# Gate and up of each layer's first feed-forward part by seven block products

## The chip, the cores and the metric

The kernel runs on one core of a Trainium2 chip. TensorE (PE) multiplies, with weight loads shown as PEld; VectorE (DVE), ScalarE (ACT) and GpSimd (POOL) do elementwise work; SyncE (SP) issues most transfers. The metric is device time in microseconds. Three runs of the kernel before took 2079.54, 2082.31 and 2081.96 us; the median is 2081.96.

## The reference

Two layers, each of four residual updates on x (512 tokens, 1024 features, float32):

```python
x = x + 0.5 * _swiglu(_rms_norm(x, norm_ffn1[l]), ffn1_w_gate[l], ffn1_w_up[l], ffn1_w_down[l])
...
x = x + mix @ w_out[l]
x = x + 0.5 * _swiglu(_rms_norm(x, norm_ffn2[l]), ffn2_w_gate[l], ffn2_w_up[l], ffn2_w_down[l])
...
def _swiglu(x, w_gate, w_up, w_down):
    return (jax.nn.silu(x @ w_gate) * (x @ w_up)) @ w_down
```

D_FF is 2816. The mixer between the two feed-forward parts (recurrent heads, windowed attention, convolution) is not touched.

## The kernel before, in words

x lies transposed in SBUF: eight tiles x0 to x7 of 128 features by 512 tokens. Every float32 product is made of three fp32r products (mm3, L119 to L121): a matrix is split into hi (a rounded copy, by ACT) and lo (the rest, a subtraction by DVE), and hi·hi, hi·lo and lo·hi are added up in PSUM.

A feed-forward part walks over f, the 22 blocks of 128 columns of D_FF. For each f it takes two weight tiles of 128 x 1024 (gate, then up). slot (L105) loads one on SP's queue into raw, copies hi on ACT (L112) and subtracts lo on DVE (L113). Each has 8 k-tiles x 3 = 24 matmuls of 512 columns, so an f has 48. gated (L212) multiplies both results by R, the reciprocal norm of each token (DVE, L216 and L218), takes silu on ACT (L217), the product on POOL (L219), and splits it into ah and al (L124, L125). Then down: for each of the eight x tiles, 22 k-tiles x 3 matmuls in three loads, the sum added to x by DVE (L271).

The norm is put off: xh and xl are x times the norm's gains (norm_tile: ACT L172, DVE L173), and squares are summed on POOL (L181); norm_sum (L199) adds them over features, and norm_spread makes R. Since R is needed only at the gating, f = 0 can be multiplied before R is known. For the next part norm_tile runs tile by tile as down finishes each x.

At the start of layer 0 the loads are raw, x0, raw, x1 to x7; PE takes gate and up of f = 0 side by side, k-tile by k-tile, as xh and xl come in.

The order of work on each engine is settled when the kernel is built, by a scheduler that simulates it; every engine and every queue then takes its instructions in that order. Tiles with a fixed number of buffers (raw, hi and lo have three each) are handed on when their last reader is done.

Of the kernel before, what the change touches and what calls it, by code (L numbers as in the profile page):

```python
# [81 lines left out]
class Kern:  # L82
# [22 lines left out]
    def slot(self, src, cols, nm="w"):  # L105

        nc = self.nc
        raw = self.ring.tile([P, 1024], F32, tag="raw", name=self.n("raw"))
# [3 lines left out]
        nc.scalar.copy(hi[:, :cols], raw[:, :cols])  # L112
        nc.vector.tensor_tensor(lo[:, :cols], raw[:, :cols], hi[:, :cols].bitcast(F32), op=ALU.subtract)  # L113
# [42 lines left out]

    def norm_begin(self, idx):
        self.xp = self.tc.tile_pool(name=self.n("xp"), bufs=1, side="right")
        pool = self.xp.__enter__()
        xh = lambda j: pool.tile([P, T], F32R, tag=f"xh{j}", name=self.n("xh"))  # L160
        xl = lambda j: pool.tile([P, T], F32R, tag=f"xl{j}", name=self.n("xl"))
        self.xh, self.xl = [xh(j) for j in range(KT)], [xl(j) for j in range(KT)]
        pool.tile([P, XPAD], F32, name=self.n("xpad"))
        self.nidx = idx
        self.acc = self.nrm.tile([P, T], F32, tag="acc", name=self.n("acc"))

    def norm_tile(self, j):
# [4 lines left out]
        nc.scalar.activation(self.xh[j], x, AF.Copy, scale=g)  # L172
        nc.vector.scalar_tensor_tensor(  # L173
            self.xl[j], x, g, self.xh[j].bitcast(F32), op0=ALU.mult, op1=ALU.subtract
        )
        if j == 0:
            nc.scalar.activation(self.acc, x, AF.Square)
        else:
            sq = self.nrm.tile([P, T], F32, tag=("sq", "R")[j % 2], name=self.n("sq"))
            nc.scalar.activation(sq, x, AF.Square)  # L180
            nc.gpsimd.tensor_tensor(self.acc, self.acc, sq, op=ALU.add)  # L181
# [41 lines left out]

    def ffn(self, l, n, nxt, last=False):
        nc, I = self.nc, self.I
        with self.tc.tile_pool(name=self.n("ffn"), bufs=1) as ap, self.tc.tile_pool(name=self.n("fft"), bufs=2) as tp:
            ah, al = [], []
            held = None
            for f in range(FT):
                p = []  # L230
                if f == 0 and l == 0 and n == 0:

                    both = [self.ahead.pop(0) for w in range(2)]
                    p = [self.psum() for w in range(2)]
# [4 lines left out]
                    self.norm_sum()
                    held = p  # L240
                    continue
                for w in range(2):
# [795 lines left out]
    def run(self):  # L1038
        nc, tc, I = self.nc, self.tc, self.I
        self.consts()  # L1040
        self.x = []
        for j in range(KT):
            if j in (0, 1):
                self.ahead.append(self.slot(I["wgu"][0, 0, 0, j], 1024))
            self.x.append(self.xt(j))
            nc.sync.dma_start(out=self.x[j], in_=I["xT"][:, j])
# [85 lines left out]
```

## Time and profile before

| | us |
|---|---|
| median of three runs | 2081.96 |
| the profiled run's own time | 2079.0 |
| its span, first to last instruction | 2077.2 |
| PE busy | 2033.1 (98%) |
| DVE busy | 1122.4 (54%) |
| ACT busy | 743.7 (36%) |
| POOL busy | 335.5 (16%) |

A window row gives a stretch's start and end, its length, the busy time of PE, PEld, DVE, ACT and POOL with their instructions in brackets, the granted PE clock, the share of the DMA engines and their GB/s. A timeline row gives a start, a duration, the engine, the line, the operation, output<-inputs, shapes and count, and in square brackets the idle time before it with what ended it. A group row (by line and form) gives busy time and the mean in ns of one after the bar.

### The profile page before, as it was taken

How to read it: one execution, taken by the hardware profiler on the slowest of the kernel's cores; microseconds unless marked ns; L12 is line 12 of the kernel's file. 1: busy time of each engine (PE TensorE's matmuls, PEld its weight loads, DVE VectorE, ACT ScalarE, POOL GpSimd, SP SyncE). 2: the span in 40 equal slices, each digit the busy share in tenths (PEclk: the TensorE clock that was granted, in tenths of full speed). 3: DMA queues.
4: the chain of work that ended last, by engine and by line, in shares of the span. 5: the costliest groups of instructions: out<-in, count | busy, mean ns of one | idle time of the engine just before them, and what ended most of it. 6: DMA issues, size and time to landing. Idle time of an engine off the chain costs nothing. (4 is left out here: it accounts for less than half of the span.)

```text
span 2077.2 us, 26018 instructions
## 1 busy us (share of the span) xinstructions
PE 2033.1 (98%) x10406; PEld 1654.5 (80%) x10406; DVE 1122.4 (54%) x1565; ACT 743.7 (36%) x1136; POOL 335.5 (16%) x298
## 2 busy tenths in 40 slices
PE   8999999989999999999999999999899999999999
PEld 6888888768877788888888888887687677888887
DVE  5545433699766455543244554337997764454422
ACT  4332322454365332322232322325534653232221
POOL 3101101132411211110010111002323111110100
PEclk9999999999999999999999999999999999999999
DMA  4232333213212323233323232332133132333332
GB/s 169 92 102 93 95 109 124 80 57 92 78 42 89 109 92 99 94 97 100 98 91 102 92 101 89 120 112 90 44 92 90 33 105 92 94 100 102 99 109 66
DMA packets 81865, 193.80 MB, mean 93 GB/s; under 512 B 26640, under 2 KB 32272, under 8 KB 81744
## 3 DMA queue, kind: packets, MB, share of 16 engines
q1 hardware_dynamic: 81312, 191.79, 29.7%
q8 instruction: 81, 1.33, 0.3%
q10 hardware_dynamic: 432, 0.36, 0.1%
q14 instruction: 40, 0.33, 0.1%
HBM read 183.47 MB, written 8.65 MB: 92 GB/s over the span
## 5 line engine op out<-in xcount | busy, mean ns | idle before, releaser
L112 ACT CAST hi<-raw 128x1024 fp32r<-128x1024 f32 (+3 forms) x368 | 350.9, 954 | 991.0 <-PE psg L120 850.0
L113 DVE TENSOR_TENSOR lo<-raw,hi 128x1024 fp32r<-128x1024 f32 (+3 forms) x368 | 504.1, 1370 | 348.7 <-ACT hi L112 329.2
L119 PE MATMUL psg<-xh,hi 128*128 128x512 f32 x1632 | 642.9, 394 | 7.1 <-ACT xh L172 7.1
L120 PE MATMUL psg<-xl,hi 128*128 128x512 f32 x1632 | 641.1, 393 | 5.0 <-DVE xl L173 4.9
L121 PE MATMUL psg<-xh,lo 128*128 128x512 f32 x1632 | 641.0, 393 | 0.0
L120 PEld LDWEIGHTS psg<-xl,hi 128*128 128x128 f32 x1632 | 308.6, 189 | 74.3 <-DVE xl L173 8.9
L119 PEld LDWEIGHTS psg<-xh,hi 128*128 128x128 f32 x1632 | 308.6, 189 | 73.8 <-ACT xh L172 7.1
L121 PEld LDWEIGHTS psg<-xh,lo 128*128 128x128 f32 x1632 | 308.8, 189 | 66.4 <-issue 2.0
L119 PE MATMUL psg<-ah,hi 128*128 128x512 f32 x704 | 273.9, 389 | 0.0
L120 PE MATMUL psg<-al,hi 128*128 128x512 f32 x704 | 273.9, 389 | 0.0
L121 PE MATMUL psg<-ah,lo 128*128 128x512 f32 x704 | 273.9, 389 | 0.0
L219 POOL TENSOR_TENSOR s<-s,u 128x512 f32<-128x512 f32 x88 | 120.5, 1370 | 800.1 <-ACT hi L112 676.5
L218 DVE TENSOR_TENSOR u<-psg,R 128x512 f32<-128x512 f32 x88 | 60.8, 691 | 265.4 <-PE psg L121 265.1
L120 PEld LDWEIGHTS psg<-al,hi 128*128 128x128 f32 x704 | 132.2, 188 | 27.5
L121 PEld LDWEIGHTS psg<-ah,lo 128*128 128x128 f32 x704 | 132.2, 188 | 27.5
L119 PEld LDWEIGHTS psg<-ah,hi 128*128 128x128 f32 x704 | 132.2, 188 | 27.3
L216 DVE TENSOR_TENSOR g<-psg,R 128x512 f32<-128x512 f32 x88 | 60.8, 691 | 125.4 <-PE psg L121 125.4
L181 POOL TENSOR_TENSOR acc<-acc,sq 128x512 f32<-128x512 f32 x42 | 58.6, 1396 | 381.3 <-ACT sq L180 380.9
L1001 DVE SCALAR_TENSOR_TENSOR cacc<-z,par,cacc 128x482 f32<-128x482 f32 (+14 forms) x120 | 101.7, 847 | 1.7
L124 ACT CAST ah<-s 128x512 fp32r<-128x512 f32 x88 | 54.8, 623 | 121.7 <-POOL s L219 121.7
L125 DVE TENSOR_TENSOR al<-s,ah 128x512 fp32r<-128x512 f32 x88 | 59.8, 679 | 20.9 <-ACT ah L124 20.9
L867 PE MATMUL psg<-hi,xh 128*128 128x384 f32 x192 | 68.0, 357 | 1.3 <-ACT nat L892 1.3
(208 smaller groups left out, 1819.2 us busy)
## 6 DMA issues: line engine op xcount, KB each, us to landing
raw<-in_wgu_dram SPq DMA_DIRECT2D x176, 512.0 KB, 3.5
raw<-in_wd_dram SPq DMA_DIRECT2D x64, 512.0 KB, 3.5
raw<-in_win_dram SPq DMA_DIRECT2D x28, 512.0 KB, 3.5
raw<-in_wd_dram SPq DMA_DIRECT2D x32, 384.0 KB, 3.1
raw<-in_watt_dram SPq DMA_DIRECT2D x24, 384.0 KB, 3.0
raw<-in_wout_dram SPq DMA_DIRECT2D x28, 192.0 KB, 2.3
xs<-x SPq DMA_DIRECT2D x16, 256.0 KB, 2.0
x<-xs SPq DMA_DIRECT2D x16, 256.0 KB, 3.1
```

Of the source, the lines that this page charges most:

```text
L112: nc.scalar.copy(hi[:, :cols], raw[:, :cols])
L113: nc.vector.tensor_tensor(lo[:, :cols], raw[:, :cols], hi[:, :cols].bitcast(F32), op=ALU.subtract)
L119: mm(out, lhsT=whi, rhs=xhi, start=first, stop=False)
L120: mm(out, lhsT=whi, rhs=xlo, start=False, stop=False)
L121: mm(out, lhsT=wlo, rhs=xhi, start=False, stop=last)
L125: self.nc.vector.tensor_tensor(lo, src, hi.bitcast(F32), op=ALU.subtract)
L181: nc.gpsimd.tensor_tensor(self.acc, self.acc, sq, op=ALU.add)
L216: nc.vector.tensor_tensor(t[0], p[0], self.R, op=ALU.mult)
L218: nc.vector.tensor_tensor(t[1], p[1], self.R, op=ALU.mult)
L219: nc.gpsimd.tensor_tensor(t[2], t[2], t[1], op=ALU.mult)
L867: mm(o, lhsT=self.xh[kk][:, t], rhs=hi[:, s], start=kk == 0, stop=False)
L1001: nc.vector.scalar_tensor_tensor(a[:, d:], z[:, 0 : T - d], pa("dww", u * CW + j), a[:, d:], op0=ALU.mult, op1=ALU.add)
```

## The change

It concerns gate and up of the first feed-forward part of each layer. The second keeps the old scheme in ffn2, which now takes odd x tiles before even ones for gate's first half, since the weights' layout in memory changed.

The tokens are cut in two halves of 256 (t0, t1) and the k-tiles in even (e) and odd (o) ones. Per f the weights are four blocks of 128 x 512: a and b (gate, even and odd), c and d (up, even and odd). Instead of eight block products (four blocks, two token halves) seven are made, each of a sum of weight blocks with a form, a sum or difference of x's blocks: 4 k-tiles x 3 matmuls of 256 columns each, 84 per f. DVE adds the seven PSUM results up to gate (negated; silu then has scale -1) and up.

norm_forms replaces norm_tile's xh and xl here: for each pair of x tiles seven forms, as fh and fl. The weights go through stages, three items ahead: stage 1 (load) loads ba (b, a), s13 (a, c) and for two f at once dd (d) on SP. Stage 2 (sums1) adds (c, d) to s13 by an accumulating DMA from POOL's queue, and makes hi and lo of ba; lo is -hi by ACT to which a second accumulating DMA from POOL's queue adds ba (only the very first by DVE). Stage 3 (sums2) makes s24 by two DVE additions and hi and lo of s13 and s24; odd makes those of dd. The items are: up for f = 0 to 7, down with those eight for all x tiles, up 8 to 15, down, up 16 to 21, down with six. Each down adds its half of the sum to x, so x is added to three times. At the start of layer 0, ba, s13 and dd are loaded before x. The seven weight sums and forms of f = 0 are multiplied in the order 1, 5, then 6, 7, 2, 3 for three of the four pairs, then the fourth pair.

```diff
+HT = T // 2
+KP = KT // 2
+CH = 8
+ER = 3
+ES = 4
...
+        if idx % 3:
+            xh = lambda j: pool.tile([P, T], F32R, tag=f"xh{j}", name=self.n("xh"))
+            xl = lambda j: pool.tile([P, T], F32R, tag=f"xl{j}", name=self.n("xl"))
+            self.xh, self.xl = [xh(j) for j in range(KT)], [xl(j) for j in range(KT)]
+        else:
+            self.fh = [pool.tile([P, 7, HT], F32R, name=self.n("fh")) for _ in range(KP)]
+            self.fl = [pool.tile([P, 7, HT], F32R, name=self.n("fl")) for _ in range(KP)]
+            self.eo = pool.tile([P, 2, 2, HT], F32, name=self.n("eo"))
+            room = room or (lambda: pool.tile([P, T], F32, name=self.n("tf")))
+            self.tf = [room().rearrange("p (a c) -> p a c", a=2) for _ in range(2)]
         pool.tile([P, XPAD], F32, name=self.n("xpad"))
...
+    def norm_forms(self, j):
+        nc = self.nc
+        V, A = nc.vector, nc.scalar
+        g = self.nidx * KT + j
+        e, o, tf = self.eo[:, 0], self.eo[:, 1], self.tf
+        h, l = self.fh[j // 2], self.fl[j // 2]
+        f32 = lambda a: a.bitcast(F32)
+        x3 = self.x[j].rearrange("p (t c) -> p t c", t=2)
+        if j % 2 == 0:
+            A.activation(e, x3, AF.Copy, scale=self.gains[:, g : g + 1])
+            A.activation(h[:, 0], e[:, 0], AF.Copy, scale=-1.0)
+            V.tensor_tensor(tf[0][:, 0], e[:, 1], e[:, 0], op=ALU.subtract)
+            A.copy(h[:, 3], tf[0][:, 0])
+            V.scalar_tensor_tensor(l[:, 0], e[:, 0], -1.0, f32(h[:, 0]), op0=ALU.mult, op1=ALU.subtract)
+            V.tensor_tensor(l[:, 3], tf[0][:, 0], f32(h[:, 3]), op=ALU.subtract)
+        else:
+            A.activation(o, x3, AF.Copy, scale=self.gains[:, g : g + 1])
+            V.tensor_tensor(tf[0][:, 1], o[:, 1], tf[0][:, 0], op=ALU.subtract)
+            V.tensor_tensor(tf[1][:, 0], e[:, 1], o[:, 1], op=ALU.subtract)
+            V.tensor_tensor(tf[1][:, 1], o[:, 0], tf[0][:, 1], op=ALU.subtract)
+            A.activation(h[:, 1:3], o, AF.Copy, scale=-1.0)
+            V.scalar_tensor_tensor(l[:, 1:3], o, -1.0, f32(h[:, 1:3]), op0=ALU.mult, op1=ALU.subtract)
+            for a, t in ((slice(4, 5), tf[0][:, 1:2]), (slice(5, 7), tf[1])):
+                A.copy(h[:, a], t)
+                V.tensor_tensor(l[:, a], t, f32(h[:, a]), op=ALU.subtract)
...
-            self.xl[j], x, g, self.xh[j].bitcast(F32), op0=ALU.mult, op1=ALU.subtract
-        )
...
+            self.norm_forms(j)
         if j == 0:
...
+    def load(self, l, n, f):
+        w, k = self.I["wgu"], KP * P
+        v = lambda a: a.rearrange("p (x k) -> p x k", x=2)
+        ba = v(self.ring.tile([P, 1024], F32, tag="raw", name=self.n("ba")))
+        self.nc.sync.dma_start(out=ba, in_=v(w[l, n, f, :, 0 : 2 * k]))
+        s13 = self.ep.tile([P, 2, k], F32, tag="rs", name=self.n("s13"), bufs=ER)
+        self.nc.sync.dma_start(out=s13, in_=v(w[l, n, f, :, k : 3 * k]))
+        if f % 2 == 0:
+            self.dd = self.ep.tile([P, 2, k], F32, tag="rd", name=self.n("dd"))
+            self.nc.sync.dma_start(out=self.dd, in_=w[l, n, f : f + 2, :, 3 * k : 4 * k].rearrange("f p k -> p f k"))
+        return {"raw": (l, n, f, ba, s13), "dd": self.dd}
+    def parts(self, hi, lo, raw, dma=False):
+        nc = self.nc
+        nc.scalar.copy(hi, raw)
+        if dma:
+            nc.scalar.activation(lo, hi.bitcast(F32), AF.Copy, scale=-1.0)
+            nc.gpsimd.dma_start(out=lo, in_=raw, accum_op=ALU.add)
+        else:
+            nc.vector.tensor_tensor(lo, raw, hi.bitcast(F32), op=ALU.subtract)
+        return hi, lo
+    def two(self, pool, tag, bufs):
+        return [
+            pool.tile([P, 2, KP * P], F32R, tag=q + tag, name=self.n(q + tag), bufs=bufs)
+            for q in ("h", "l")
+        ]
+    def sums1(self, W):
+        l, n, f, ba, s13 = W["raw"]
+        k = KP * P
+        cd = self.I["wgu"][l, n, f, :, 2 * k : 4 * k].rearrange("p (x k) -> p x k", x=2)
+        self.nc.gpsimd.dma_start(out=s13, in_=cd, accum_op=ALU.add)
+        h, lo = (
+            self.ring.tile([P, 1024], F32R, tag=q, name=self.n(q), bufs=RB).rearrange("p (x k) -> p x k", x=2)
+            for q in ("hi", "lo")
+        )
+        self.parts(h, lo, ba, W["dma"])
+        W[1] = h[:, 1], lo[:, 1], 0
+        W[2] = h[:, 0], lo[:, 0], 1
+    def sums2(self, W):
+        V = self.nc.vector
+        l, n, f, ba, s13 = W["raw"]
+        s24 = self.ep.tile([P, 2, KP * P], F32, tag="rs", name=self.n("s24"), bufs=ER)
+        V.tensor_tensor(s24[:, 0], s13[:, 1], ba[:, 1], op=ALU.add)
+        V.tensor_tensor(s24[:, 1], s24[:, 0], ba[:, 0], op=ALU.add)
+        h, lo = self.parts(*self.two(self.ep, "s", ES), s13)
+        W[5] = h[:, 1], lo[:, 1], 3
+        W[7] = h[:, 0], lo[:, 0], 5
+        h, lo = self.parts(*self.two(self.ep, "s", ES), s24)
+        W[6] = h[:, 0], lo[:, 0], 4
+        W[3] = h[:, 1], lo[:, 1], 2
+    def odd(self, W):
+        f = W["raw"][2]
+        if f % 2 == 0:
+            self.hdd = self.parts(*self.two(self.ep, "d", 1), W["dd"])
+        W[4] = self.hdd[0][:, f % 2], self.hdd[1][:, f % 2], 6
...
+            def gated(f, g, u):
+                V.tensor_tensor(g, g, self.R, op=ALU.mult)
+                A.activation(g, g, AF.Silu, scale=-1.0)
+                V.tensor_tensor(u, u, self.R, op=ALU.mult)
+                G.tensor_tensor(g, g, u, op=ALU.mult)
+                ah[f] = ap.tile([P, T], F32R, tag=f"ah{f % CH}", name=self.n("ah"))
+                al[f] = ap.tile([P, T], F32R, tag=f"al{f % CH}", name=self.n("al"))
+                self.split(ah[f], al[f], g)
+            def up(f, W, held, then):
+                ps = {}
+                def mul(i, r=range(KP)):
+                    if i not in ps:
+                        ps[i] = self.psum(*(("b", 2) if i in (2, 7) else ()))[:, 0:HT]
+                    hi, lo, c = W[i]
+                    for p in r:
+                        s = slice(p * P, (p + 1) * P)
+                        self.mm3(ps[i], hi[:, s], lo[:, s], self.fh[p][:, c], self.fl[p][:, c], p == 0, p == KP - 1)
+                add = lambda o, i, z: V.tensor_tensor(o, ps[i], z, op=ALU.add)
+                g, u = (tp.tile([P, T], F32, tag=q, name=self.n(q)) for q in "gu")
+                (g0, g1), (u0, u1) = ((z[:, 0:HT], z[:, HT:]) for z in (g, u))
+                self.odd(W)
+                mul(1)
+                A.copy(g0, ps[1])
+                mul(5)
+                if f == 0:
+                    for i in (6, 7, 2, 3):
+                        mul(i, range(KP - 1))
+                    r = [KP - 1]
+                else:
+                    r = range(KP)
+                mul(6, r)
+                add(u1, 6, g0)
+                add(g1, 5, u1)
+                if f == 1:
+                    self.norm_spread()
+                if held:
+                    gated(*held)
+                mul(7, r)
+                add(u0, 7, u1)
+                add(u1, 5, u0)
+                then()
+                mul(2, r)
+                add(g0, 2, g0)
+                mul(3, r)
+                add(g1, 3, g1)
+                mul(4)
+                add(u0, 4, u0)
+                if f == 0:
+                    return f, g, u
+                gated(f, g, u)
+            def down(j, q, m, W):
+                end = q + m == FT
+                ps = self.psum()
+                hi, lo = W
+                for k in range(m):
+                    s = slice(k * P, (k + 1) * P)
+                    self.mm3(ps, hi[:, s], lo[:, s], ah[q + k], al[q + k], k == 0, k == m - 1)
+                V.scalar_tensor_tensor(self.x[j], ps, 0.5, self.x[j], op0=ALU.mult, op1=ALU.add)
+                if not end:
+                    return
+                self.norm_tile(j)
+                nc.sync.dma_start(out=self.xs[:, j], in_=self.x[j])
+            items = []
+            for q in range(0, FT, CH):
+                m = min(CH, FT - q)
+                items += [("up", f, q, m) for f in range(q, q + m)] + [("down", j, q, m) for j in range(KT)]
...
+            W = {}
+            def stage(k, i):
+                if i >= len(items):
+                    return
+                kind, z, q, m = items[i]
+                if kind == "up":
+                    if k == 1:
+                        W[i] = self.load(l, n, z)
+                        W[i]["dma"] = i > 0 or l > 0
+                    elif k == 2:
+                        self.sums1(W[i])
+                    else:
+                        self.sums2(W[i])
+                elif k == 1:
+                    W[i] = self.raw(I["wd"][l, n, z, :, q * P : (q + m) * P], m * P)
+                elif k == 3:
+                    W[i] = self.ready(W[i], m * P)
+            held = None
+            stage(1, 0)
+            stage(2, 0)
+            if self.late:
+                self.late()
+                self.late = None
+            stage(1, 1)
+            stage(3, 0)
+            stage(2, 1)
+            stage(1, 2)
+            for i, (kind, z, q, m) in enumerate(items):
+                stage(2, i + 2)
+                if kind == "up":
+                    held = up(z, W.pop(i), held, lambda: stage(3, i + 1))
+                    if z == 0:
+                        self.norm_sum()
+                else:
+                    if (z, q + m) == (0, FT):
+                        self.norm_close()
+                        self.norm_begin(nxt)
+                    stage(3, i + 1)
+                    down(z, q, m, W.pop(i))
+                stage(1, i + 3)
...
-                    hi, lo = self.ahead.pop(0) if self.ahead else self.slot(I["wgu"][l, n, f, w], 1024)
+                    hi, lo = self.slot(I["wgu"][l, n, f, :, 2 * w * KP * P : 2 * (w + 1) * KP * P], 1024)
                     ps = self.psum()
                     for k in range(KT):
+                        z = (k % KP) * 2 + (k // KP + w + 1) % 2
                         s = slice(k * P, (k + 1) * P)
-                        self.mm3(ps, hi[:, s], lo[:, s], self.xh[k], self.xl[k], k == 0, k == KT - 1)
+                        self.mm3(ps, hi[:, s], lo[:, s], self.xh[z], self.xl[z], k == 0, k == KT - 1)
                     p.append(ps)
...
-                self.norm_begin(nxt)
+                self.norm_begin(nxt, lambda: tp.tile([P, T], F32, tag="s", name=self.n("tf")))
...
-        self.consts2()
+        def late():
+            for j in range(KT):
+                self.x.append(self.xt(j))
+                nc.sync.dma_start(out=self.x[j], in_=I["xT"][:, j])
+            for j in range(KT):
+                self.norm_tile(j)
+            self.consts2()
+        self.late = late
         for l in range(self.depth):
             self.ffn(l, 0, 3 * l + 1)
             self.mixer(l)
-            self.ffn(l, 1, 3 * l + 3 if l + 1 < self.depth else None, last=l + 1 == self.depth)
+            self.ffn2(l, 1, 3 * l + 3 if l + 1 < self.depth else None, last=l + 1 == self.depth)
...
+    gu = gu.reshape(L, 2, 2, KP, 2, P, FT, P).transpose(0, 1, 6, 2, 4, 5, 3, 7).reshape(L, 2, FT, 4, P, KP * P)
```

Where instructions moved, first on PE at the start of layer 0. Before (psg_186 is gate, psg_187 up), f = 0 starts and ends so:

```order
1 L119 MATMUL psg_186<-xh_119,hi_88 128x512
2 L120 MATMUL psg_186<-xl_127,hi_88 128x512
3 L121 MATMUL psg_186<-xh_119,lo_89 128x512
4 L119 MATMUL psg_187<-xh_119,hi_96 128x512
5 L120 MATMUL psg_187<-xl_127,hi_96 128x512
6 L121 MATMUL psg_187<-xh_119,lo_97 128x512
7 L119 MATMUL psg_186<-xh_120,hi_88 128x512
```

After, the end of product 1 (psg_270), and what follows (psg_284, 297 and psb_307, 317 are products 5, 6, 7 and 2; hs and ls are the parts of s13 and s24):

```order
10 L131 MATMUL psg_270<-fh_94,hi_120 128x256
11 L132 MATMUL psg_270<-fl_98,hi_120 128x256
12 L133 MATMUL psg_270<-fh_94,lo_121 128x256
13 L249 MATMUL psc_380<-ones,acc_103 128x1 x4
14 L131 MATMUL psg_284<-fh_91,hs_238 128x256
15 L132 MATMUL psg_284<-fl_95,hs_238 128x256
16 L131 MATMUL psb_307<-fh_91,hs_238 128x256
17 L132 MATMUL psb_307<-fl_95,hs_238 128x256
18 L131 MATMUL psb_317<-fh_91,hi_120 128x256
19 L132 MATMUL psb_317<-fl_95,hi_120 128x256
```

L249 is norm_sum's; it stood behind the 48th matmul of f = 0, and stands behind the twelfth of 84.

DVE at the same place, before (xl of the last tiles, then rnt, in norm_sum, and later weights):

```order
9 L173 SCALAR_TENSOR_TENSOR xl_132<-x_109,gains,xh_124 128x512
10 L173 SCALAR_TENSOR_TENSOR xl_133<-x_111,gains,xh_125 128x512
11 L173 SCALAR_TENSOR_TENSOR xl_134<-x_113,gains,xh_126 128x512
12 L113 TENSOR_TENSOR lo_245<-raw_243,hi_244 128x1024
13 L185 TENSOR_SCALAR rnt<-psc_236 128x4
14 L113 TENSOR_TENSOR lo_283<-raw_281,hi_282 128x1024
```

and after, where the last forms are made (fl_98, the fourth pair):

```order
40 L212 TENSOR_TENSOR fl_98<-tf_100,fh_94 128x256
41 L212 TENSOR_TENSOR fl_98<-tf_101,fh_94 128x512
42 L235 TENSOR_SCALAR rnt<-psc_380 128x4
43 L283 TENSOR_TENSOR ls_239<-s_19_115,hs_238 128x1024
44 L283 TENSOR_TENSOR ls_243<-s_40_235,hs_242 128x1024
45 L311 TENSOR_TENSOR s_62_347<-s_39_233,ba_231 128x512
46 L312 TENSOR_TENSOR s_62_347<-s_62_347,ba_231 128x512
```

The parts ls of both weight sums and the sum s_62 (s24 of the next f) stand behind the last form and rnt.

SP where layer 1 begins, before:

```order
235 L111 DMA raw_7903<-in_wd_dram 128x1024
236 L111 DMA raw_7933<-in_wd_dram 128x768
237 L111 DMA raw_7971<-in_wgu_dram 128x1024
238 L111 DMA raw_8002<-in_wgu_dram 128x1024
239 L111 DMA raw_8040<-in_wgu_dram 128x1024
```

and after:

```order
246 L117 DMA raw_9336<-in_wd_dram 128x1024
247 L117 DMA raw_9366<-in_wd_dram 128x768
248 L268 DMA ba_9415<-in_wgu_dram 128x1024
249 L268 DMA ba_9427<-in_wgu_dram 128x1024
250 L268 DMA ba_9448<-in_wgu_dram 128x1024
251 L270 DMA s_1651_9417<-in_wgu_dram 128x1024
252 L273 DMA dd_9419<-in_wgu_dram 128x2x512
253 L270 DMA s_1656_9429<-in_wgu_dram 128x1024
254 L273 DMA dd_9452<-in_wgu_dram 128x2x512
```

Behind the last down weights two raw tiles per f came in turn; now three ba come first, then s13 (s_1651), dd, the next s13. The first s13 lies on memory that ffn2 of layer 0 used, and waits for PE, DVE and POOL.

More of the change, by code (lines that the diff above doesn't have):

```diff
@@ L107, in slot, with raw, ready @@
         nc = self.nc
+        return self.ready(self.raw(src, cols), cols)
+    def raw(self, src, cols):
         raw = self.ring.tile([P, 1024], F32, tag="raw", name=self.n("raw"))
+        self.wdma = self.nc.sync.dma_start(out=raw[:, :cols], in_=src)
+        return raw
+    def ready(self, raw, cols):
+        nc = self.nc
         hi = self.ring.tile([P, 1024], F32R, tag="hi", name=self.n("hi"), bufs=RB)
         lo = self.ring.tile([P, 1024], F32R, tag="lo", name=self.n("lo"), bufs=RB)
-        self.wdma = nc.sync.dma_start(out=raw[:, :cols], in_=src)
         nc.scalar.copy(hi[:, :cols], raw[:, :cols])
@@ L155, in tb, with norm_begin @@
         return self.tab[:, TAB[n][0] : TAB[n][1]]
-    def norm_begin(self, idx):
+    def norm_begin(self, idx, room=None):
         self.xp = self.tc.tile_pool(name=self.n("xp"), bufs=1, side="right")
         pool = self.xp.__enter__()
-        xh = lambda j: pool.tile([P, T], F32R, tag=f"xh{j}", name=self.n("xh"))
-        xl = lambda j: pool.tile([P, T], F32R, tag=f"xl{j}", name=self.n("xl"))
-        self.xh, self.xl = [xh(j) for j in range(KT)], [xl(j) for j in range(KT)]
+        if idx % 3:
[8 more added lines that the diff above has]
+            self.tf = [room().rearrange("p (a c) -> p a c", a=2) for _ in range(2)]
         pool.tile([P, XPAD], F32, name=self.n("xpad"))
@@ L170, in norm_tile @@
         x = self.x[j]
-        g = self.gains[:, self.nidx * KT + j : self.nidx * KT + j + 1]
-        nc.scalar.activation(self.xh[j], x, AF.Copy, scale=g)
-        nc.vector.scalar_tensor_tensor(
-            self.xl[j], x, g, self.xh[j].bitcast(F32), op0=ALU.mult, op1=ALU.subtract
-        )
+        if self.nidx % 3:
+            g = self.gains[:, self.nidx * KT + j : self.nidx * KT + j + 1]
+            nc.scalar.activation(self.xh[j], x, AF.Copy, scale=g)
+            nc.vector.scalar_tensor_tensor(
+                self.xl[j], x, g, self.xh[j].bitcast(F32), op0=ALU.mult, op1=ALU.subtract
+            )
+        else:
+            self.norm_forms(j)
         if j == 0:
@@ new lines, in parts @@
+    def parts(self, hi, lo, raw, dma=False):
+        nc = self.nc
+        nc.scalar.copy(hi, raw)
[10 more added lines that the diff above has]
+        ]
@@ new lines, in sums1 @@
+    def sums1(self, W):
[6 more added lines that the diff above has]
+            for q in ("hi", "lo")
+        )
+        self.parts(h, lo, ba, W["dma"])
+        W[1] = h[:, 1], lo[:, 1], 0
+        W[2] = h[:, 0], lo[:, 0], 1
@@ new lines, in odd, with ffn @@
+    def odd(self, W):
[3 more added lines that the diff above has]
+        W[4] = self.hdd[0][:, f % 2], self.hdd[1][:, f % 2], 6
+    def ffn(self, l, n, nxt):
+        nc, I = self.nc, self.I
+        V, A, G = nc.vector, nc.scalar, nc.gpsimd
+        with (
+            self.tc.tile_pool(name=self.n("ffn"), bufs=1) as ap,
+            self.tc.tile_pool(name=self.n("fft"), bufs=2) as tp,
+            self.tc.tile_pool(name=self.n("ext"), bufs=1) as self.ep,
+        ):
+            ah, al = [None] * FT, [None] * FT
+            def gated(f, g, u):
[97 more added lines that the diff above has]
+                        self.norm_sum()
+                else:
+                    if (z, q + m) == (0, FT):
[4 more added lines that the diff above has]
+                stage(1, i + 3)
@@ L222, in gated, with ffn2 @@
         self.split(ah[f], al[f], t[2])
-    def ffn(self, l, n, nxt, last=False):
+    def ffn2(self, l, n, nxt, last=False):
         nc, I = self.nc, self.I
@@ L1041, in run @@
         self.x = []
[L1042 to L1046, printed above, removed]
         self.xs = self.dp.tile([P, KT, T], F32, name="xs")
         self.norm_begin(0)
-        for j in range(KT):
-            self.norm_tile(j)
-        self.consts2()
+        def late():
[6 more added lines that the diff above has]
+        self.late = late
         for l in range(self.depth):
```

12 lines of the change are left out of this document (1 added, 11 removed).

## The prediction

> **What bounds the kernel now.** I read the page's engine line first, then the windows over the feed-forward stretches, then single rows of the timeline. The engine line says that PE works in 98% of the span; no other engine comes near.
>
> ```profile
> PE 2033.1 (98%) x10406; PEld 1654.5 (80%) x10406; DVE 1122.4 (54%) x1565; ACT 743.7 (36%) x1136; POOL 335.5 (16%) x298
> 24.00:232.00 208.00, 208.00 (x923) 172.39 (x922) 104.94 (x98) 63.44 (x78) 27.22 (x20) 1.00 0.32 102
> 939.00:1060.00 121.00, 121.00 (x540) 100.32 (x540) 37.04 (x40) 32.77 (x40) 11.64 (x8) 1.00 0.32 98
> ```
>
> The two window rows (length, then PE, PEld, DVE, ACT, POOL busy, granted clock, DMA share, GB/s) lie in gate and up of layer 0 and over the end of layer 0 with the start of layer 1. PE is busy for all of both at clock 1.00, with DVE at half and DMA at a third. So these stretches last as long as their matmuls, and what the change does to them is matmul time plus whatever new waiting it brings. The pace of a matmul:
>
> ```profile
> 100.00 0.39 PE L120 MATMUL psg<-xl,hi 128*128 128x512 f32 x1
> 100.68 0.39 PE L120 MATMUL psg<-xl,hi 128*128 128x512 f32 x1
> 498.24 0.33 PE L867 MATMUL psg<-hi,xh 128*128 128x384 f32 x1
> 498.76 0.33 PE L867 MATMUL psg<-hi,xh 128*128 128x384 f32 x1
> 401.19 0.97 PEld L436 LDWEIGHTS psb<-tab,tmp 128*128 128x128 f32 x8 [0.90 <-ACT tmp L433]
> 402.07 0.19 PEld L121 LDWEIGHTS psg<-xh,lo 128*128 128x128 f32 x1
> ```
>
> Each pair of matmul rows is three apart: 0.68/3 = 0.2267 us for 512 columns, 0.52/3 = 0.1733 for 384, so 0.0533 per 128 columns and 0.0133 fixed; 256 columns come to 0.120. The records (0.39, 0.33) overlap and are no pace. Eight weight loads took 0.97; with one load's 0.19 taken off, seven starts in 0.78 are 0.111 each, the floor for a matmul with its own load.
>
> **The matmul term.** Per f, 48 matmuls of 512 columns become 84 of 256. Before, f repeats every 10.88 us:
>
> ```profile
> 100.65 0.69 DVE L218 TENSOR_TENSOR u<-psg,R 128x512 f32<-128x512 f32 x1 [3.31 <-PE psg L121]
> 111.53 0.69 DVE L218 TENSOR_TENSOR u<-psg,R 128x512 f32<-128x512 f32 x1 [3.31 <-PE psg L121]
> ```
>
> After: 84 x 0.120 = 10.08. That is 0.80 per f; 21 f after the first one in each of two layers give 42 x 0.80 = **-33.6**. Its best end is the load floor, 84 x 0.111 = 9.32, or -65.5; its other end is 0.1295 (three quarters of what 384 columns take), where 84 need the old 10.88, so 0. I take the line through the two sizes.
>
> **Start of layer 0.** This is where new work stands in front of PE with nothing to hide it.
>
> ```profile
> 7.13 0.79 PE L119 MATMUL psg<-xh,hi 128*128 128x512 f32 x1 [7.13 <-ACT xh L172]
> 7.95 1.04 ACT L112 CAST hi<-raw 128x1024 fp32r<-128x1024 f32 x1 [0.36 <-DMA raw<-in_wgu_dram]
> 10.17 10.94 DVE L173 SCALAR_TENSOR_TENSOR xl<-x,gains,xh 128x512 fp32r<-128x512 f32 x7
> 10.22 12.04 POOL L181 TENSOR_TENSOR acc<-acc,sq 128x512 f32<-128x512 f32 x7 [8.54 <-ACT sq L180]
> 22.43 0.95 PE L199 MATMUL psc<-ones,acc 128*128 128x1 f32 x8
> 23.49 2.36 DVE L113 TENSOR_TENSOR lo<-raw,hi 128x1024 fp32r<-128x1024 f32 x2
> 4.00:8.00 4.00, 0.87 (x2) 0.37 (x2) 1.98 (x2) 2.33 (x4) 0.00 (x0) 1.00 1.02 370
> 8.00:12.00 4.00, 3.96 (x8) 2.32 (x9) 2.97 (x3) 3.89 (x6) 1.78 (x1) 1.00 1.06 400
> L113 DVE TENSOR_TENSOR lo<-raw,hi 128x256 fp32r<-128x256 f32 x12 | 5.1, 424 | 2.9 <-ACT hi L112 2.9
> L125 DVE TENSOR_TENSOR al<-s,ah 128x512 fp32r<-128x512 f32 x88 | 59.8, 679 | 20.9 <-ACT ah L124 20.9
> ```
>
> Before, f = 0 was done at 22.4, when norm_sum starts. DVE rows abut with a small overlap: two of 1024 in 2.36 with a single one at 1.23 makes 1.13 from one to the next. With the same 0.1 off, 256 columns cost 0.33 and 512 about 0.58 to 0.60.
>
> Two raw tiles and one x (1.25 MB) had landed by 7.95. Now ba, s13, dd and x0 (1.75 MB) come first; 0.52 MB more at 400 GB/s is 1.3, so x0 is there near 9.3. DVE reaches the forms at about 10.8, after the parts of ba and dd. A pair of x tiles needs seven instructions of 256 and two of 512 (norm_forms), 7 x 0.34 + 2 x 0.60 = 3.6; four pairs 14.4. s24 adds 2 x 0.6 = 1.2. POOL's seven squares run against them: before, seven xl took 10.94 instead of 7 x 0.60 = 4.2, so each POOL add cost DVE (10.94 - 4.2)/7 = 0.96; seven again 6.7. DVE has the last form at 10.8 + 14.4 + 1.2 + 6.7 = 33.1, and then rnt and ls_239 (row 43 of its order), 34.3. PE's order puts norm_sum, which waits for POOL's last square, ahead of products 5, 6, 7, 2 and 3, so nearly all of the other 72 matmuls come after 34.3: 8.6 us, and about 1.5 for the slow clock after a gap (rows below): f = 0 ends near 44, **+22**. Bounds: with half the POOL cost and 3.0 per pair, 38.5, +16; with every DVE row at its full record, +27.
>
> **Start of layer 1.** Before, the last x of layer 0 is written at 1042.60 and f = 0 is through at 1053.29, without a gap in PE:
>
> ```profile
> 1042.60 0.69 DVE L271 SCALAR_TENSOR_TENSOR x<-psg,x 128x512 f32<-128x512 f32 x1 [1.95 <-PE psg L121]
> 1053.29 0.95 PE L199 MATMUL psc<-ones,acc 128*128 128x1 f32 x8
> raw<-in_wgu_dram SPq DMA_DIRECT2D x176, 512.0 KB, 3.5
> L112 ACT CAST hi<-raw 128x1024 fp32r<-128x1024 f32 x268 | 282.0, 1052 | 813.6 <-PE psg L120 723.8 <-issue 82.4 <-DMA raw<-in_wgu_dram 4.0
> ```
>
> Now the first s13 load on SP waits for PE and DVE to leave ffn2's memory; behind it on SP stand dd and the second s13. From PE's last matmul: last forms 5.5; the load 3.5; the accumulate, for which no row exists, at 3.5 as a plain transfer plus 1 for its issue; cast 1.05; ls 1.2: product 5 can run at about 15.5. Then about 72 x 0.120 = 8.6 and 1.5 of slow clock: 25.6 instead of 10.9, **+15**. Bounds +10 (forms at 4, no issue cost, part of product 2 done in the gap) and +20 (an accumulate of twice a load). The slow clock and its price:
>
> ```profile
> 684.73 0.74 PE L120 MATMUL psg<-xl,hi 128*128 128x512 f32 x1 [1.95 <-DVE xl L173]
> 685.27 0.63 PE L121 MATMUL psg<-xh,lo 128*128 128x512 f32 x1
> 685.70 0.63 PE L119 MATMUL psg<-xh,hi 128*128 128x512 f32 x1
> 688.25 0.40 PE L119 MATMUL psg<-xh,hi 128*128 128x512 f32 x1
> ```
>
> After a 1.95 us gap the matmuls stand 0.43 apart until 688.25: eight at 0.2 lost, some 1.6. The Trainium skill (TensorE: Matmul & The Clock Gate, The HAM clock gate) has the array at half rate until it was busy for about 3.4 us; these rows agree, with 3.5.
>
> **Smaller terms.** ffn2 now takes odd x tiles first, so x7 is needed some matmuls earlier behind the same xl: +0.7 per layer, **+1.4**. The last part of down has six k-tiles behind gate and up of f = 21, whose al comes last: **+1**, between 0 and 4.
>
> **Does PE stay the bound?** Per f on DVE: seven adds 7 x 0.34 = 2.4, two products with R 1.2, al 0.6, s24 1.2, two ls 2.3, half of ld 0.6, together 8.3, and the lock of one POOL product:
>
> ```profile
> 101.51 1.29 POOL L219 TENSOR_TENSOR s<-s,u 128x512 f32<-128x512 f32 x1 [9.59 <-ACT hi L112]
> 101.55 2.33 DVE L113 TENSOR_TENSOR lo<-raw,hi 128x1024 fp32r<-128x1024 f32 x1 [0.21 <-ACT hi L112]
> 106.99 1.23 DVE L113 TENSOR_TENSOR lo<-raw,hi 128x1024 fp32r<-128x1024 f32 x1 [0.21 <-ACT hi L112]
> ```
>
> The same subtraction takes 2.33 beside POOL and 1.23 alone, so 1.1: 9.4 of 10.08. It just fits, but DVE works in order and al waits for POOL and ACT; where it is late, psum comes free late. DMA: 1.31 MB plain at the start's 385 GB/s are 3.4 us, and 1.05 MB accumulated are 2.7k, where k is an accumulated byte's price over a plain one's; no row shows k. At k = 1 it is 6.1, and the bound is reached at k = 2.45. I add 0.1 per f for both, **+4** (0 to 15).
> The Trainium skill (Collectives: The Full Stack, The bandwidth ceiling) says that an add in the DMA engines needs two source reads, twice the traffic of a copy; by that k = 2 and 8.8 us, still under 10.08. No row before shows it.
>
> **Sum** for the profiled run of 2079.0: -33.6 + 22 + 15 + 1.4 + 1 + 4 = +9.8, so 2088.8; the median of the runs shown, 2081.96, stands 3.0 above that run: **2092**.
>
> **Rivals.** (a) *Faster*: the starts cost their lower ends and steady stretches nothing: -33.6 + 16 + 10 + 1.4 = -6, 2076. Going further, the load floor as pace takes another 32: 2044. For it: half of f = 0's matmuls need only what is early; against it: norm_sum stands ahead of them in PE's order. (b) *DVE becomes the bound*: each f has two accumulates issued on POOL; should an issue shut DVE out as a POOL product does, for 1.0 each, DVE needs 11.4 per f, and the gain turns into 42 x 1.3 = 55 more, in place of the 4: 2143; it decides from about 0.35 per issue. For it the 2.33 row; against it, no POOL DMA is in this trace. In the Trainium skill (DMA: Bandwidth & Descriptors, SWDGE vs HWDGE vs iDMA) GpSimd writes the descriptors of such transfers into SBUF state from which DVE can shut it out, which is this mechanism seen from POOL. (c) *DMA becomes the bound*: k = 3 makes 11.5 per f, 42 x 1.4 = 60 more in place of the 4: 2148; from k = 2.45 on.
>
> **How the numbers follow.** About 0.2% (4 us) is what a measurement here can tell from no change. Chances: my sum 0.46, with an own range of 2080 to 2104 (about half of the way to each term's bounds); (a) 0.30, of which the load floor 0.06; (b) 0.14; (c) 0.10. No measurable change is the low edge of my sum's range, up to 2086, 0.16, and (a)'s upper edge, 0.04: 0.20. Faster is the rest of (a), 0.26; slower the rest of my sum, 0.30, with (b) and (c): 0.54. The range leaves out the load floor and most of (c): 2064 to 2142.
>
> **What would show it.** Matmuls of 256 columns 0.120 apart, f every 10.1; norm_sum of layer 0 near 33 and f = 0 ending near 44; in layer 1 a PE gap of 6 to 9 us before product 5, released by ls or hs behind the s13 accumulate. Wrong if PE shows gaps in every f behind psum (then b or c: see whether DVE is full, or the accumulates land late), or if f = 0 of layer 0 ends before 36.

## The result, and the profile after

The changed kernel takes 2166.49 us (median of 2162.91 to 2170.97) beside 2081.3 of the kernel before: a ratio of 1.0417, 95% interval 1.0402 to 1.0433. It is slower, as forecast, but by 85 us where I had 10, and outside of the range (2064 to 2142). Single runs of one kernel scatter here by some 5 us to either side (thirteen of the kernel before on one chip: 2076.3 to 2086.8), so differences below that are read from points of the traces, not from times.

The page's engine line of the changed kernel, and its window rows over two gate and up stretches of layer 0 (f = 8 to 15, f = 16 to 21; columns as before):

```profile
PE 2037.4 (94%) x11990; PEld 1727.0 (80%) x11990; DVE 1315.1 (61%) x2072; ACT 876.3 (40%) x1329; POOL 416.8 (19%) x385
182.00:278.00 96.00, 85.11 (x669) 83.77 (x669) 63.04 (x109) 40.98 (x54) 19.61 (x19) 0.95 0.74 177
323.00:390.00 67.00, 64.47 (x513) 62.45 (x511) 44.55 (x80) 28.32 (x39) 14.52 (x17) 1.00 0.57 136
```

PE, busy throughout before, now stands still for 11 of the 96 us of the first row, where its granted clock is 0.95, while DVE has a third of its time free. So nothing is simply full. The ledger, by the start of the last addition into x of each part:

| part | before | after | difference |
|---|---|---|---|
| layer 0, first feed-forward | 372.65 | 420.07 | +47.4 |
| layer 0, mixer and second | 669.95 | 669.22 | -0.7 |
| layer 1, first feed-forward | 360.92 | 400.76 | +39.8 |
| layer 1, mixer and second | 670.05 | 675.41 | +5.4 |

The last row holds work that the change leaves alone, but for the order of the x tiles in ffn2; in the eleven other kernels below the two such parts take 666.8 to 675.5, so 5.4 is within what they scatter. The profiled run of the change took 2171.0, so its ledger adds up to 92 and not to 85. Within the first feed-forward parts, by the count of its 84 matmuls, f = 0 of layer 0 ends at 45.9 instead of 22.4 (+23.5), f = 0 of layer 1 30.8 after PE's last matmul of layer 0 instead of 10.9 (+20), and the 21 other f with their down items take 374.2 and 370.2 instead of 350.2 each: +24 and +20, where the matmul term alone would make -17 each. What is lost there comes to **some 77 us**, against 4 in my sum.

Matmuls of 256 columns, eleven apart (timeline of PE):

```profile
57.99 0.28 PE L132 MATMUL psb<-fl,hi 128*128 128x256 f32 x1
59.31 0.28 PE L131 MATMUL psg<-fh,hs 128*128 128x256 f32 x1
```

1.32/11 = 0.120. And one of the stalls, at the end of f = 9, from the timelines of SP, POOL, ACT, DVE and PE in order of time:

```profile
191.39 0.38 SPq L270 DMA_DIRECT2D s<-in_wgu_dram  x1
201.73 0.88 POOL L297 DMA_DIRECT2D s<-in_wgu_dram  x1 [10.09 <-DMA s<-in_wgu_dram]
202.29 1.61 POOL L340 TENSOR_TENSOR g<-g,u 128x512 f32<-128x512 f32 x1
203.93 0.62 ACT L136 CAST ah<-g 128x512 fp32r<-128x512 f32 x1 [10.87 <-POOL g L340]
204.58 0.69 DVE L137 TENSOR_TENSOR al<-g,ah 128x512 fp32r<-128x512 f32 x1 [9.84 <-ACT ah L136]
205.19 0.42 DVE L357 TENSOR_TENSOR u<-psg,g 128x256 f32<-128x256 f32 x1
205.66 0.58 PE L131 MATMUL psg<-fh,hi 128*128 128x256 f32 x1 [4.37 <-DVE u L357]
```

Read from the bottom: PE waits for a psum buffer that a DVE addition empties; that addition stands behind al; al waits for ah, ah for the product g·u on POOL; and the product, whose inputs were long there, stands on POOL behind the accumulating transfer, which for 10.09 us waited for s13's load to land. An issue that waits holds up the work queued behind it on its engine.

### The profile page after: what moved, and what is told of

It reads as the page before. It is cut to its first block, busy times and chain, and to the rows that moved or that the text cites. A ratio compares the mean times of both kernels' runs of the same rounds, so it can differ in the third digit from the quotient of the medians.

```text
span 2169.2 us, 30167 instructions
## 1 busy us (share of the span) xinstructions
PE 2037.4 (94%) x11990; PEld 1727.0 (80%) x11990; DVE 1315.1 (61%) x2072; ACT 876.3 (40%) x1329; POOL 416.8 (19%) x385
## 3 DMA queue, kind: packets, MB, share of 16 engines
q0 software_dynamic: 12528, 45.62, 11.3%
## 5 line engine op out<-in xcount | busy, mean ns | idle before, releaser
L125 DVE TENSOR_TENSOR lo<-raw,hi 128x1024 fp32r<-128x1024 f32 (+3 forms) x280 | 353.2, 1261 | 171.3 <-ACT hi L124 161.0
L131 PE MATMUL psg<-xh,hi 128*128 128x512 f32 x928 | 367.7, 397 | 1.8 <-ACT xh L220 1.8
L132 PE MATMUL psg<-xl,hi 128*128 128x512 f32 x928 | 365.6, 394 | 3.7 <-DVE xl L221 3.7
L133 PE MATMUL psg<-xh,lo 128*128 128x512 f32 x928 | 366.3, 395 | 0.2
L132 PEld LDWEIGHTS psg<-xl,hi 128*128 128x128 f32 x928 | 176.0, 190 | 43.1 <-DVE xl L221 4.6
L131 PEld LDWEIGHTS psg<-xh,hi 128*128 128x128 f32 x928 | 175.6, 189 | 40.9 <-issue 2.5
L133 PEld LDWEIGHTS psg<-xh,lo 128*128 128x128 f32 x928 | 176.2, 190 | 39.3 <-issue 2.0
L131 PE MATMUL psg<-fh,hs 128*128 128x256 f32 x528 | 157.8, 299 | 30.7 <-DVE g L357 11.9
L132 PE MATMUL psg<-fl,hs 128*128 128x256 f32 x528 | 154.4, 292 | 0.0
L133 PE MATMUL psg<-fh,ls 128*128 128x256 f32 x528 | 153.7, 291 | 0.0
L131 PEld LDWEIGHTS psg<-fh,hs 128*128 128x128 f32 x528 | 106.6, 202 | 36.2 <-DVE g L357 15.5
L283 DVE TENSOR_TENSOR ls<-s,hs 128x1024 fp32r<-128x1024 f32 x88 | 108.8, 1241 | 13.2 <-ACT hs L278 12.9
```

Of the source, the lines that this page charges most:

```text
L131: mm(out, lhsT=whi, rhs=xhi, start=first, stop=False)
L132: mm(out, lhsT=whi, rhs=xlo, start=False, stop=False)
L133: mm(out, lhsT=wlo, rhs=xhi, start=False, stop=last)
L283: nc.vector.tensor_tensor(lo, raw, hi.bitcast(F32), op=ALU.subtract)
```

## Experiments

Each edit is against the changed kernel or the one named; all times are beside 2079.6 to 2081.2 of the kernel before on the same chip. gu_dve was run twice (2124.4 and 2135.5) and starts ten times, the others once. The order of work is settled anew for each edit, so work that an edit doesn't name can move too; the table at the end of this section reads the effect from the traces.

**gu_dve.** The product leaves POOL.

```diff
-                G.tensor_tensor(g, g, u, op=ALU.mult)
+                V.tensor_tensor(g, g, u, op=ALU.mult)
```

> The product of gate and up (L340) moves from POOL to DVE; POOL then holds only transfers in these stretches. Theory Q (in POOL's order the product stands behind an accumulating transfer that waits for s13's load, so al comes late, DVE's later adds too, and PE waits for psum): the waits in the middle of gate and up go, an f takes 10.1 to 10.8 us instead of some 12.6, and the time falls by 60 or more, to 2090 to 2110. Rival D (the DMA engines bound it, the accumulates being dear): an f stays at 12 or more, the time above 2150. Rival V (DVE is full): DVE gets 0.6 more work and 1.1 less of being shut out by POOL, so the time changes by less than 15.

2129.9 us, ratio 1.0232 (1.0168 to 1.0296): 37 less than the change, where Q asked for 60 or more. V falls, and so does D as it was put: f takes 11.1 on average in the second stretch. It now takes 10.1 twice (copies of g at 188.68, 198.77, 208.84) and then 14.4 and 14.5, and what is left has another chain:

```profile
207.03 0.87 POOL L297 DMA_DIRECT2D s<-in_wgu_dram  x1 [9.36 <-DVE g L357]
215.00 0.69 DVE L311 TENSOR_TENSOR s<-s,ba 128x512 f32<-128x512 f32 x1 [5.44 <-issue]
218.06 0.39 PE L131 MATMUL psg<-fh,hi 128*128 128x256 f32 x1 [0.62 <-DVE u L357]
176.00:265.00 89.00, 85.13 (x685) 83.16 (x685) 70.23 (x120) 43.38 (x55) 10.50 (x12) 1.00 0.84 195
```

The accumulate issued at 207.03 lands some 8 us later, and only then can DVE make s24 from s13 (L311; the profile names no releaser); the psum additions queue behind it. The DMA share is 0.84.

**plain_dma** and **no_accumulate.** The accumulating transfers made plain, and left out.

```diff
-        self.nc.gpsimd.dma_start(out=s13, in_=cd, accum_op=ALU.add)
+        self.nc.gpsimd.dma_start(out=s13, in_=cd)
...
-            nc.gpsimd.dma_start(out=lo, in_=raw, accum_op=ALU.add)
+            nc.gpsimd.dma_start(out=lo.bitcast(F32), in_=raw)
```

> Both accumulating transfers become plain ones of the same bytes from the same queue with the same waits (so s13 and lo hold other numbers). Theory Q: the waits for s13's load stay in POOL's queue, only somewhat shorter with less traffic: 2120 to 2150. Rival D: the extra read of an accumulate was the bound, so an f falls to 10.1 to 10.5 and the time to 2085 to 2100. In both, the landing of such a transfer tells the price of accumulating (7.5 and 8.3 us with it).

> Both accumulating transfers are left out (s13 lacks its second half, lo is only -hi). Theories Q and D: no wait in POOL's queue and 1 MB less per f, so an f takes 10.1 to 10.4; the start of layer 1 loses its 8.2 us accumulate too: 2070 to 2090. If an f stays above 11.5, the stall has another cause (DVE's order, psum), and both theories fall.

2113.3 and 2086.0 us. The first lies between the two theories: each holds a part. The transfers' price, in the changed kernel and with plain ones (queue row: packets, MB, share of the span; issue rows: median us to landing):

```profile
q0 software_dynamic: 12528, 45.62, 11.3%
s<-in_wgu_dram POOLq DMA_DIRECT2D x44, 512.0 KB, 7.5
lo<-ba POOLq DMA_DIRECT2D x43, 512.0 KB, 8.3
```

```profile
q0 software_dynamic: 12528, 45.62, 6.0%
s<-in_wgu_dram POOLq DMA_DIRECT2D x44, 512.0 KB, 4.8
lo<-ba POOLq DMA_DIRECT2D x43, 512.0 KB, 4.9
```

The same bytes take 11.3% of 2169.2 = 245 us of the DMA engines against 6.0% of 2111.5 = 127: **k = 1.93**. Without the transfers f takes 10.0 to 10.2 on average in the later stretches, so no third cause of that size is left there.

**dve_plain.** Both edits together.

> The product on DVE and both accumulating transfers plain (other numbers in s13 and lo). It takes away POOL's queue and the accumulates' price together, leaving waits and bytes. If these two are all of the stall, an f takes 10.1 to 10.3 and the time 2085 to 2097. If it stays above 2105, something third holds PE, and the order on DVE is the first to look at.

2086.8 us. The stretches from f = 8 on run at 10.0 to 10.1 per f on average. Queue and accumulate together are the stall.

**ring5.** gu_dve, and:

```diff
-ER = 3
-ES = 4
+ER = 5
+ES = 3
```

> On top of the product on DVE: five buffers instead of three for s13 and s24 (ER), and three instead of four for their parts (ES), which frees the room. Theory L (a loop: with three buffers s13 of f + 2 can be loaded only when s24 of f is done, and load 6.4, accumulate 7.6, two additions, cast and parts make some 20 us for two f, whatever the engines could do): f falls from 11.0 to 10.1 to 10.4, the time from 2130 to 2095 to 2110. Rival D2 (the DMA engines are simply busy, share 0.84 in these stretches): less than 8 us.

2108.3 us, 22 less than gu_dve, with the same bytes and the same price per byte. f is down to 10.0 to 10.2 on average in all but the first stretch. The window over f = 8 to 15 of layer 0:

```profile
170.00:253.00 83.00, 82.23 (x677) 81.53 (x676) 68.38 (x116) 43.62 (x55) 11.42 (x13) 1.00 0.78 191
```

PE works in 82.2 of 83 us. So the DMA engines were not the bound at gu_dve's 0.84: it was the loop of load, accumulate and additions through three buffers. D2 falls. The start of layer 0 is 5 us longer here (f = 0 ends at 51.1 instead of 46.1), so the loop alone is worth more than the 22.

**lo_dve.** gu_dve, and lo of ba always by DVE:

```diff
-                        W[i]["dma"] = i > 0 or l > 0
+                        W[i]["dma"] = False
```

> On top of the product on DVE: lo of ba by DVE's subtraction instead of -hi and an accumulating transfer. DMA loses half of its accumulating (2.6 us per f at 1.93 times a plain byte), DVE gets 1.13 more, 10.0 of 10.08. Theories L and D2: s13's load and accumulate land 2 us earlier and f comes to 10.3 to 10.8, the time to 2095 to 2115. If DVE's order is the limit instead, f stays at 11 or more: 2130 or above.

2099.0 us, 31 less than gu_dve. Copies of g in f = 9 and f = 15 of layer 0, and the windows of the second and third stretch:

```profile
177.99 0.37 ACT L362 COPY g<-psg 128x256 f32<-128x256 f32 x1 [1.95 <-PE psg L133]
238.47 0.37 ACT L362 COPY g<-psg 128x256 f32<-128x256 f32 x1 [2.73 <-PE psg L133]
168.00:238.00 70.00, 70.00 (x585) 70.00 (x585) 64.51 (x106) 33.58 (x42) 5.20 (x6) 1.00 0.61 161
292.00:346.00 54.00, 54.00 (x452) 54.00 (x451) 47.19 (x79) 23.53 (x31) 1.73 (x2) 1.00 0.36 96
```

60.48/6 = 10.08, the forecast pace to the hundredth, PE busy throughout, and that with DVE busy for 64.5 of 70 us. So DVE has room for the product and the subtraction, and off POOL's queue they cost less. s13's accumulate now lands after 5.8 instead of 7.6.

**no_squares.** POOL's additions of squares left out ahead of the changed parts.

```diff
-            nc.gpsimd.tensor_tensor(self.acc, self.acc, sq, op=ALU.add)
+            if self.nidx % 3:
+                nc.gpsimd.tensor_tensor(self.acc, self.acc, sq, op=ALU.add)
```

> POOL's seven additions of squares are left out in the norms ahead of the changed parts (so R is wrong there). My sum gave each 0.96 us of DVE: in layer 0 the last form comes 6 to 7 us earlier, near 28.5 instead of 35.3, and f = 0 ends by as much earlier; in layer 1 one such addition meets forms at the end, 1 us. Together 7 to 9 us less, 2157 to 2160. If DVE's forms don't move, POOL's part in the start is nothing and the forms' own time is all of it.

2148.4 us, 18 less, where 7 to 9 were expected. At the start of layer 0 the copy of g of f = 0 comes at 34.04 instead of 40.04, the 6 that the sum gave to POOL. Of the 22.6 between the profiled runs, another 9 arise in later f of layer 0 (the part takes 405.1 instead of 420.1) and 8.6 in the last row of the ledger, where this edit changes nothing; why those f are shorter stays open. The layer 1 part takes 401.6, as with the change.

**x_first_acc.** gu_dve, and at the start of layer 0 x is loaded behind ba, with the squares added on DVE:

```diff
         self.nc.sync.dma_start(out=ba, in_=v(w[l, n, f, :, 0 : 2 * k]))
+        if self.late:
+            late, self.late = self.late, None
+            late()
...
-            if self.late:
-                self.late()
-                self.late = None
...
-            nc.gpsimd.tensor_tensor(self.acc, self.acc, sq, op=ALU.add)
+            (nc.gpsimd if self.nidx else nc.vector).tensor_tensor(self.acc, self.acc, sq, op=ALU.add)
```

> On top of the product on DVE, at the start of layer 0 only: x is loaded before s13 and dd, and the seven additions of squares go to DVE (0.6 each) instead of POOL. By my sum for the start: forms begin 4.5 us earlier, at 6.8 instead of 11.3, and 6.7 of being shut out become 4.2: the last form at about 28, f = 0 ends 7 us earlier, and the time falls from 2130 to 2119 to 2126. If the forms' end doesn't move, x's landing and POOL weren't what set the start.

2117.1 us, 13 less than gu_dve (4 to 11 expected); the copy of g of f = 0 moves from 39.72 to 29.94, 9.8 earlier. Direction and place are right, the size is somewhat larger.

**ring_l1.** lo_dve, and in layer 1 s13 of f = 0 by two plain loads into raw's ring (load), one addition on DVE (sums1), s24 in the same ring (sums2):

```diff
+        if f == 0 and l > 0:
+            s13 = v(self.ring.tile([P, 1024], F32, tag="raw", name=self.n("s13")))
+            W["cd"] = v(self.ring.tile([P, 1024], F32, tag="raw", name=self.n("cd")))
+            self.nc.sync.dma_start(out=W["cd"], in_=v(w[l, n, f, :, 2 * k : 4 * k]))
...
+        if "cd" in W:
+            self.nc.vector.tensor_tensor(s13, s13, W["cd"], op=ALU.add)
...
+        s24 = W["cd"] if "cd" in W else self.ep.tile([P, 2, KP * P], F32, tag="rs", name=self.n("s24"), bufs=ER)
```

> On top of lo_dve (product and lo on DVE): in layer 1 alone, f = 0 gets s13 by two plain loads into raw's ring, which is free before the end of layer 0, and one addition on DVE; s24 lies in the ring too. That takes the wait for ffn2's memory with the load (4.5) and the accumulate (8.2) out of the start of layer 1; only the casts into that memory still wait. By my reading product 5 starts 8 to 10 us after PE's last matmul of layer 0 instead of 19.3, and the time falls from 2099 by 8 to 12, to 2087 to 2091. If the memory wait alone sets it, the gap stays above 15 and the gain is under 4.

2087.3 us, 12 less; product 5 of layer 1 starts 8.3 after PE's last matmul, as expected, and the layer's own part takes 359.0 instead of 365.7, so 7 of it are shown to lie there.

**starts** joins lo_dve, x_first_acc and ring_l1.

> Everything together: product and lo on DVE, x first and squares added on DVE at the start of layer 0, s13 of layer 1's first f by plain loads. The terms found so far add up to 2099 - 13 - 10 = 2076, 2072 to 2082, which is at or a little below the kernel before (2080). It would show that the matmul term (-33.6) stands and that the rest of the miss was waits: an f of 10.08 in all six stretches. If the gains don't add (DVE has 10.0 us of work in 10.08), 2083 to 2092.

2078.0 us (median of ten) beside 2080.0 (of thirteen), ratio 0.9996 (0.9982 to 1.001): no measurable difference from the kernel before. The last additions into x fall at 372.36 in layer 0 (before: 372.65), and layer 1's part takes 360.64 (360.92). Starts of product 5 in layer 0 and layer 1:

```profile
23.43 0.58 PE L131 MATMUL psg<-fh,hs 128*128 128x256 f32 x1 [0.53 <-ACT hs L287]
1051.63 0.56 PE L131 MATMUL psg<-fh,hs 128*128 128x256 f32 x1
```

They stood at 35.44 and 1108.47, the latter 19.4 after PE's last matmul, now 8.5. What the seven products save in 21 f is here just what their first f costs, in each layer: f = 0 takes 13.2 and 7.2 more than before, the 21 others 13.5 and 7.5 less. Of the 16.8 per layer that the matmul term gives, 3 and 9 still go to waits. f is 10.08 on average in the second and third stretch of each layer; the waits lie in the first ones, so the expectation of all six isn't met.

**starts5** is starts with the buffers of ring5.

> The same with five buffers for s13 and s24 and three for their parts. If the first stretch of layer 0 (f = 1 to 7, 10.3 to 12.5 us per f in the earlier runs) is still held by the loop over three buffers, 3 to 8 us less than starts; if by DVE or by hs and ls, no change or a few us more.

2083.9 us in one run: no gain that can be told. The first part ends at 370.1 instead of 372.4, the layer 1 part takes 362.1 instead of 360.6.

What the 21 f after the first lose, read from each trace as in the ledger (from the end of f = 0 to the start of the last addition into x, less the 350.2 - 16.8 = 333.4 that the matmul term gives):

| run | layer 0 | layer 1 | both |
|---|---|---|---|
| the change | 40.7 | 36.7 | 77 |
| gu_dve | 22.8 | 11.0 | 34 |
| plain_dma | 15.5 | 13.9 | 29 |
| lo_dve | 5.1 | 3.8 | 9 |
| dve_plain | 5.1 | -0.1 | 5 |
| ring5 | 5.2 | -0.9 | 4 |
| no_accumulate | 2.5 | 1.2 | 4 |

The starts don't enter here. The product on DVE takes 43 of the 77 away, and five buffers 30 of the 34 that are left, with every accumulate still made.

## Why the prediction was wrong

- **Matmul term: right.** 0.120 us for 256 columns, and f = 10.08 wherever nothing stalls. The load floor of 0.111 didn't show.
- **Start of layer 0: right**, +23.5 against +22 (16 to 27). The chain is nearly what it was to be (PE, DVE and PE of the changed kernel):

```profile
32.89 1.86 PE L249 MATMUL psc<-ones,acc 128*128 128x1 f32 x8 [0.67 <-POOL acc L231]
34.31 1.01 DVE L212 TENSOR_TENSOR fl<-tf,fh 128x256 fp32r<-128x256 f32 x2
35.44 0.58 PE L131 MATMUL psg<-fh,hs 128*128 128x256 f32 x1 [0.68 <-ACT hs L278]
```

  norm_sum comes at 32.9 for "near 33", and the end at 45.9 for 44. The last form ends at 35.3 where the sum had 33.1; in return product 5 doesn't wait for ls, as the sum had it, but for hs of ACT.
- **Start of layer 1: right in mechanism, its accumulate mis-sized**, +20 against +15, at the edge of its bounds:

```profile
1094.57 0.33 SPq L270 DMA_DIRECT2D s<-in_wgu_dram  x1
1099.16 0.87 POOL L297 DMA_DIRECT2D s<-in_wgu_dram  x1 [2.61 <-DMA s<-in_wgu_dram]
1107.37 1.04 ACT L278 CAST hs<-s 128x1024 fp32r<-128x1024 f32 x1 [5.14 <-DMA s<-in_wgu_dram]
1108.47 0.58 PE L131 MATMUL psg<-fh,hs 128*128 128x256 f32 x1 [10.67 <-ACT hs L278]
```

  The load waits until 5.5 after the last matmul, as forecast, and takes 4.6 (I had 3.5). The accumulate takes 8.2 from issue to use; I had 4.5, a plain transfer and its issue, and plain ones do land after 4.8 (plain_dma). Product 5 waits for hs alone, so the 1.2 of ls falls out.
- **The step that failed is "Does PE stay the bound?"**, with "I add 0.1 per f for both, +4 (0 to 15)". It compared the work of DVE (9.4) and of the DMA engines (6.1 to 8.8) with 10.08 and found that both fit. They do; the runs put some 77 us in place of the 4, from two waits that no count of work shows. One is POOL's order: the accumulate that waits for s13's load stands ahead of g·u, and al and the psum additions behind that (gu_dve: 37 less, and 43 of the 77). The other is the loop of load (5.4), accumulate (7.5), s24's additions, casts and parts through three buffers, in which s13 of f + 2 waits for s24 of f (ring5: 22 less with the same bytes; lo_dve: 31 less with a shorter way). The price of accumulating lengthens both: with plain transfers, and the order and the buffers as they were, 29 are lost instead of 77. The step came close to the first wait ("al waits for POOL and ACT; where it is late, psum comes free late") and gave it, with the DMA's share, 0.1 per f without a row for it. The order could have been read beforehand: stage(2, i + 2), which issues the accumulate, stands ahead of up, which makes the product, but orders were laid out for PE, DVE and SP alone.
- **Smaller terms:** at the second part's entry PE waits 2.8 in each layer instead of 2.3 and 2.5, so +0.7 in all, where +1.4 was given. Down's entries of the first part stall for 0.5 and 0.2 on ah and al at the first two of a layer, and for 0.2 at the last one, so not for the last six k-tiles alone: some 3 in all, for the +1 (0 to 4) that I gave.
- **Rivals.** (b) named DVE and POOL's issues, but with a mechanism that isn't there. The issues take 0.87 in the median, and DVE's parts beside one keep their length (timelines of POOL and DVE of the changed kernel, one beside an issue, one without):

```profile
254.24 0.88 POOL L297 DMA_DIRECT2D s<-in_wgu_dram  x1 [2.69 <-DMA s<-in_wgu_dram]
254.43 1.21 DVE L283 TENSOR_TENSOR ls<-s,hs 128x1024 fp32r<-128x1024 f32 x1
257.36 1.21 DVE L283 TENSOR_TENSOR ls<-s,hs 128x1024 fp32r<-128x1024 f32 x1
```

  The Trainium skill (DMA: Bandwidth & Descriptors, SWDGE vs HWDGE vs iDMA) says that DVE can lock GpSimd out there while it is in its 2-port mode; no run here shows that: the issue takes 0.88 beside DVE's work and 0.86 without it. (c) needed k of 2.45; k is 1.93. By the rule of two source reads (the Trainium skill, Collectives: The Full Stack, The bandwidth ceiling) it would be 2: the traces agree, with 1.93. (a) came true for neither start. The range, which ended at 2142, left (b)'s own 2143 just outside.

The time lies above rival (c)'s 2148 and came by another way than (c): from waiting, with the DMA share at 0.74. PE's gaps behind psum, the prediction's sign of being wrong, did come, but neither of the two rivals that it named for them (a full DVE, full DMA engines) is the cause. The direction was no luck: without the 77 the starts (+43.5) still outweigh the matmul term (-33.6), as in the sum.

## What to carry to other kernels

Before work moves to the queue of another engine to relieve a full one, write down what stands behind it there: an issue that waits for a load holds everything queued after it, and a short product behind it can stop PE. A count of work per period only bounds a pipeline from below; for each ring of buffers add up the latencies of one turn, from a load to the last reader that frees the buffer, divide by the periods that a turn serves (two f here), and compare that with the period as well. And a scheme that saves per block pays for its set-up once per entry: here 21 blocks of 0.8 us, less the 3 and 9 us that still went to waits, just covered one start (13 and 7).

## What the runs showed of the hardware

- An accumulating transfer costs 1.93 times the DMA time of a plain one of the same bytes, and landed 7.5 to 8.3 us after its issue where the plain one took 4.8 to 4.9 (medians, the change beside plain_dma). This is a mean of two kinds, from HBM and from SBUF: 5.4 us per MB for both, 6.1 where only those from HBM are left (lo_dve, 23.07 MB in 6.7% of 2096.9).
- An accumulating transfer's issue holds POOL for 0.87 us, a plain one's for 0.53 to 0.60 (plain_dma). 256-wide and 1024-wide work of DVE beside it is not lengthened, where a POOL product beside it costs DVE 1.1 (2.33 instead of 1.23, before).
- fp32r matmuls keep their line down to 256 columns (0.0533 per 128 and 0.0133), with weight loads of 128 columns for each of them.
